# First slice of b on ScalarE's queue beside the rows of a, and its cast moved between the tiles of a

## The chip, the cores and the metric

One NeuronCore of a Trainium2 chip. The time is that of one execution on the device, in microseconds (us), median of several runs. "Span" is what the profile counts, from the first to the last instruction; it is about 1.8 us shorter than the time of the same execution (121.4 and 123.2).

## The reference

```python
m, k, n, p = 1024, 1024, 2048, 1024          # a: m x k, b: k x n, c: n x p, float32
h = np.matmul(a, b)
h = 0.5 * h * (1 + np.tanh(np.sqrt(2 / np.pi) * (h + 0.044715 * h ** 3)))
return np.matmul(h, c)
```

## The kernel before

The first half of a (four row tiles of 128 x 1024, 512 KB each) is loaded, cast to bf16 in halves by VectorE and ScalarE, transposed on TensorE and evicted in halves. Then the first product runs over eight slices of b (128 rows x 768 columns, 384 KB each), cast in halves by the same two engines. All these loads go out on SyncE's queue, a's four tiles first. Some small matmuls on zeros ("warm-ups") keep TensorE busy meanwhile. The rest of the kernel is untouched by the change.

```python
    def load_b0(k):
        st = b0stage.tile([128, W0], F32, name="b0_st")
        nc.sync.dma_start(out=st, in_=bv[:, k, 0:W0])
        b_st[k] = st
    ...
    for mt in range(4):
        load_a0(mt)                      # nc.sync
    for k in range(KT):                  # KT = 8
        load_b0(k)
    ...
    warm_up(8)                           # matmuls on zeros
    ...
    ab = [cast_a0(0)]                    # half on VectorE, half on ScalarE
    for mt in range(4):
        if mt < 3:
            ab.append(cast_a0(mt + 1))
        turn0(mt, ab[mt])                # 8 transposes; evictions: 4 on VectorE, 4 on ScalarE
        if mt < 3:
            warm_up(3)
    cast_b0(0)
    for k in range(KT):
        if k + 1 < KT:
            cast_b0(k + 1)
        for t in range(N0):              # N0 = 6
            nc.tensor.matmul(ps[t], bt(k, t), aT[0][:, k, :],
                             start=(k == 0), stop=(k == KT - 1))
```

## Time and profile before

| | before |
|---|---|
| time, median of 3 runs | 124.18 us (124.11 to 124.19) |
| time and span of the profiled execution | 123.2 us, 121.4 us |
| landings of a's tiles, as seen by VectorE's casts | 4.11, 5.37, 6.85, 8.14 |
| first matmul of the first product | 10.13 |
| landing of b's second slice | 10.89 |

A landing is read from the timeline: the start of the VectorE cast that waited for it.

### The profile page before, as it was taken

The numbers are of one execution on the slowest core, as the hardware profiler recorded it, in microseconds if no ns is written. First come the engines' busy times: TensorE is split into PE (matmuls) and PEld (weight loads), VectorE is DVE, ScalarE is ACT, GpSimd is POOL, SyncE is SP. The second block draws the span as 40 slices with busy tenths as digits, with TensorE's granted clock in tenths as the row PEclk, the third lists the DMA queues.
The fourth block names the chain that finished last, engine by engine and source line by source line (L and its number), as shares of the span: only waits on it lengthen the run. The fifth ranks groups of instructions, "written<-read, shape, count | busy, mean of one in ns | idle before, by whom it ended". The sixth has DMA issues, their size and how long they took to land.

```text
span 121.4 us, 1456 instructions
## 1 busy us (share of the span) xinstructions
PE 115.0 (95%) x562; PEld 67.2 (55%) x569; DVE 64.2 (53%) x94; ACT 30.8 (25%) x54; POOL 21.3 (18%) x26
## 2 busy tenths in 40 slices
PE   6897999999998999999999999999999999999980
PEld 2353444444456444444444444478888888888850
DVE  0354320000026000009999999999669999963440
ACT  4486535417311323332333233000000000000000
POOL 2000497134420400000000000994000000000000
PEclk9999999999999999999999999999999999999997
DMA  4999999999999999992000000002400024263443
GB/s 123 393 347 337 408 219 205 200 203 207 209 205 205 386 357 213 207 207 43 0 0 5 0 0 3 3 0 88 171 0 0 5 86 153 106 224 121 173 155 104
DMA packets 12150, 18.44 MB, mean 152 GB/s; under 512 B 752, under 2 KB 7152, under 8 KB 12144
## 3 DMA queue, kind: packets, MB, share of 16 engines
q0 software_dynamic: 7968, 8.91, 40.0%
q1 hardware_dynamic: 4176, 9.44, 21.0%
q8 instruction: 4, 0.07, 0.2%
q14 instruction: 2, 0.02, 0.0%
HBM read 20.97 MB, written 4.19 MB: 207 GB/s over the span
## 4 chain that ended last, share of the span: by engine, by line
PE 89%; DMA 4%; DVE 2%; issue 1%; SPq 1%; DVEq 0%
PE ps L267 41%; PE ps L164 31%; PE ps L136 9%; DMA a_st<-in_a_dram 4%; PE ps L155 3%; PE pt L155 3%; PE pt L183 1%; PE pt L111 1%; SPq L76 1%; DVE aT L114 1%; DVE aT L184 1%; PE ps L97 1%; DVE ab L103 0%; DVEq L362 0%; DVE b_lo L121 0%
## 5 line engine op out<-in xcount | busy, mean ns | idle before, releaser
L140 ACT ACTIVATE h<-ps 128x512 fp32r<-128x512 f32 (+1 forms) x30 | 17.3, 602 | 28.7 <-PE ps L164 26.3
L164 PE MATMUL ps<-aT,b_hi 128*128 128x512 bf16 x93 | 21.2, 379 | 0.2
L164 PE MATMUL ps<-aT,b_lo 128*128 128x512 bf16 x79 | 17.4, 379 | 0.1
L164 PEld LDWEIGHTS <-b_hi 128*128 128x128 bf16 x96 | 9.3, 98 | 10.9
L267 PE MATMUL ps<-t,s 128*128 128x512 f32 x64 | 15.1, 393 | 0.0
L267 PE MATMUL ps<-t,h 128*128 128x512 f32 x64 | 14.8, 389 | 0.0
L267 PE MATMUL ps<-c,h 128*128 128x512 bf16 (+2 forms) x71 | 14.1, 355 | 0.1
L267 PEld LDWEIGHTS ps<-t,s 128*128 128x128 f32 x64 | 12.0, 188 | 2.6
L267 PEld LDWEIGHTS ps<-t,h 128*128 128x128 f32 x64 | 12.0, 188 | 2.5
L307 POOL COPY lk<-u 128x512 f32<-128x512 f32 x1 | 7.5, 7492 | 33.6 <-ACT u L300 33.6
L164 PEld LDWEIGHTS <-b_lo 128*128 128x128 bf16 x80 | 7.8, 98 | 9.5
L221 DVE TENSOR_TENSOR t<-c,c 128x1024 fp32r<-128x1024 bf16 x4 | 4.7, 1222 | 15.6 <-ACT h L140 15.5
L184 DVE COPY aT<-pt 128x1024 bf16<-128x1024 bf16 x4 | 2.7, 689 | 19.4 <-PE pt L183 19.3
L136 PE MATMUL ps<-aT,b_lo 128*128 128x512 bf16 x47 | 10.3, 379 | 0.7 <-DVE b_lo L121 0.7
L267 PEld LDWEIGHTS <-h 128*128 128x128 bf16 x72 | 6.7, 98 | 7.4 <-issue 0.3
L209 POOL DMA_DIRECT2D c<-in_c_dram x8 | 5.9, 743 | 11.8 <-PE ps L164 6.0
L136 PEld LDWEIGHTS <-b_lo 128*128 128x128 bf16 x48 | 4.5, 98 | 6.1 <-DVE b_lo L121 0.8
L290 DVE TENSOR_TENSOR ot<-ps,u 128x512 f32<-128x512 f32 x11 | 7.3, 685 | 1.1 <-PE ps L267 1.1
L267 PE MATMUL ps<-c,s 128*128 128x512 f32 x32 | 7.4, 389 | 0.0
L97 PE MATMUL ps<-warm 128*128 128x512 bf16 x17 | 5.7, 476 | 1.2 <-DVE warm L49 1.2
L267 PEld LDWEIGHTS ps<-c,s 128*128 128x128 f32 x32 | 6.0, 188 | 1.2
L121 DVE CAST b_lo<-b_st 128x384 bf16<-128x384 f32 x8 | 2.9, 366 | 4.5 <-DMA b_st<-in_b_dram 4.5
(40 smaller groups left out, 95.1 us busy)
## 6 DMA issues: line engine op xcount, KB each, us to landing
out_dram<-ot SPq DMA_DIRECT2D x15, 256.0 KB, 2.0
b_st<-in_b_dram SPq DMA_DIRECT2D x8, 384.0 KB, 8.7
c<-in_c_dram POOLq DMA_DIRECT2D x6, 512.0 KB, 14.6
a_st<-in_a_dram SPq DMA_DIRECT2D x4, 512.0 KB, 4.7
c<-in_c_dram POOLq DMA_DIRECT2D x2, 1024.0 KB, 15.0
b_hi<-in_b_dram POOLq DMA_DIRECT2D x4, 384.0 KB, 11.3
b_lo<-in_b_dram POOLq DMA_DIRECT2D x2, 512.0 KB, 7.1
ab<-in_a_dram POOLq DMA_DIRECT2D x4, 256.0 KB, 13.9
```

The costliest lines, as they stand in the source:

```text
L97: nc.tensor.matmul(ps[N0 - 1], warm[:, 0:128], warm, start=True, stop=True)
L121: nc.vector.tensor_copy(b_lo[:, k, 0:HW], b_st[k][:, 0:HW])
L136: nc.tensor.matmul(ps[t], bt(k, t), aT[0][:, k, :], start=(k == 0), stop=(k == KT - 1))
L140: nc.scalar.activation(hq[h][t // NH][:, t % NH, :], p, AF.Gelu_apprx_tanh)
L155: nc.tensor.matmul(ps[t], bt(k + i, N0 + t), aT[0][:, k + i, :], start=(k + i == 0), stop=(k + i == KT - 1))
L164: nc.tensor.matmul(p, bt(k, t), aT[h][:, k, :], start=(k == 0), stop=(k == KT - 1))
L184: nc.vector.tensor_copy(aT[1][:, :, ts(j, 128)], pt)
L209: nc.gpsimd.dma_start(out=dst[:, t:t + 4, :], in_=cv[:, r * NH + t:r * NH + t + 4, ts(q, H)])
L221: nc.vector.tensor_tensor(t1[i], c12[:, ts(i, 2), :], c11[:, ts(i, 2), :], op=SUB)
L267: nc.tensor.matmul(p, lhs(t)[:, ts(j, 128)], rhs(t)[:, q], start=(t == 0), stop=(t == NH - 1))
L290: nc.vector.tensor_tensor(ot, u if swap else p, p if swap else u, op=op)
L307: nc.gpsimd.tensor_copy(last_keep, last)
```

## The change

The intent: b's first slice need not queue behind a, so its cast can be done while the engines wait for a, and nothing stands between the last eviction and the first matmul.

```diff
-    def load_b0(k):
+    def load_b0(k, queue=nc.sync):
         st = b0stage.tile([128, W0], F32, name="b0_st")
-        nc.sync.dma_start(out=st, in_=bv[:, k, 0:W0])
+        queue.dma_start(out=st, in_=bv[:, k, 0:W0])
 ...
+    load_b0(0, nc.scalar)
     for mt in range(4):
         load_a0(mt)
-    for k in range(KT):
+    for k in range(1, KT):
         load_b0(k)
 ...
     for mt in range(4):
         if mt < 3:
             ab.append(cast_a0(mt + 1))
+        if mt == 1:
+            cast_b0(0)
         turn0(mt, ab[mt])
         if mt < 3:
             warm_up(3)
-    cast_b0(0)
```

## The prediction

> **What bounds the kernel now.** I read the page first: the busy shares, the sliced picture, the chain that ended last.
>
> ```profile
> PE 115.0 (95%) x562; PEld 67.2 (55%) x569; DVE 64.2 (53%) x94; ACT 30.8 (25%) x54; POOL 21.3 (18%) x26
> PEclk9999999999999999999999999999999999999997
> PE 89%; DMA 4%; DVE 2%; issue 1%; SPq 1%; DVEq 0%
> ```
>
> TensorE works for 95% of the 121.4 us span and makes 89% of the chain, at a full clock until the last slice. What is left of the chain is mostly the head: 4% is a DMA of a. So a change to the head can only move the moment at which the dense stream of matmuls starts. I read the chain in order of time up to that moment (columns: start, length, what).
>
> ```profile
> 1.65 5.18 DMA a_st<-in_a_dram
> ...
> 7.67 0.73 PE pt L111 x8
> 8.40 0.65 PE ps L97 x3
> 9.05 0.30 PE pt L111 x4
> 9.35 0.02 issue
> 9.37 0.42 DVE aT L114
> 9.80 0.28 DVE b_lo L121
> 10.07 0.27 issue
> 10.35 10.33 PE ps L136 x47
> ```
>
> The reader is to see three things. The head is paced by the row tiles of a. After the last VectorE eviction of a transposed tile (9.37 to 9.80) the cast of b's first slice adds 0.28 us before the first weights can be loaded; this is what the change takes away. And the first matmul stage then runs without a hole: the row has 47 records where the code issues 48, and the timeline puts the first weight load at 10.12 with the first recorded matmul at 10.35, one step of 0.2155 us too late. So the missing record is the first matmul, at 10.13, and "0.27 issue" is no wait. 48 x 0.2155 = 10.34 us, to 20.48, where the next stage begins. From there the chain is TensorE almost to the end, with gaps of 0.05 us.
>
> The timeline shows what the last tile of a had to go through (start, length, engine, line, and in brackets the idle time before it):
>
> ```profile
> 8.14 0.63 ACT L104 ACTIVATE ab<-a_st 128x512 bf16<-128x512 f32 x1 [0.17 <-DMA a_st<-in_a_dram]
> 8.14 0.43 DVE L103 CAST ab<-a_st 128x512 bf16<-128x512 f32 x1 [0.53 <-DMA a_st<-in_a_dram]
> ...
> 8.48 0.42 DVE L114 COPY aT<-pt 128x512 bf16<-128x512 bf16 x1
> ...
> 8.95 0.74 PE L111 MATMUL pt<-ident,ab 128*128 128x128 bf16 x8
> ...
> 10.89 0.36 DVE L121 CAST b_lo<-b_st 128x384 bf16<-128x384 f32 x1 [0.83 <-DMA b_st<-in_b_dram]
> ```
>
> The casts of tile 3 wait for its landing; the eviction of tile 2 stands behind the cast in VectorE's order; the transposes of tile 3 need the bank that this eviction frees. Landing to first matmul is 10.13 - 8.14 = 1.99 us. The last row is the second slice of b, landed at 10.89. The same view has the other landings of a at 4.11, 5.37 and 6.85, and the third slice of b at 11.89.
>
> Last, the table by stretches (engine columns, then granted clock, DMA share, GB/s):
>
> ```profile
> 4.00:8.00 4.00, 3.47 (x28) 1.79 (x27) 1.95 (x5) 2.86 (x5) 0.00 (x0) 1.00 1.01 397
> 8.00:10.25 2.25, 1.69 (x16) 1.10 (x16) 1.45 (x4) 1.64 (x4) 0.00 (x0) 1.00 0.85 224
> ```
>
> While a is on its way the 16 DMA engines are full (share 1.01, 397 GB/s). There is a weak stretch, 8.00 to 10.25 at 224 GB/s, but it lies after a has landed, while the first two slices of b arrive. I don't know its cause.
>
> **What the Trainium skill says.** "DMA: Bandwidth & Descriptors", section "Issuing engines are not separate DMA queues": transfers started from different engines run on the same 16 DMA engines and interleave, and starting them from several engines "will only save the time on the sequencer it takes to initiate the DMA". The trace of before has only one such queue busy in the head, so it can't confirm the sharing; it does show full engines. The same page, "Queues, rings and completion order", says that a DMA engine goes round robin between the queues with work, packet by packet. No run yet shows that. "ScalarE: Activation LUTs", section "What ACT_TABLE_LOAD costs", gives about 1283 ns for the load; the trace has 1.28 us at 0.74, so it agrees. "TensorE: Matmul & The Clock Gate", section "HAM oscillation — how this bites in real kernels", warns of TensorE gaps above some 3.4 us; in before the clock stays at 1.00 with short gaps only.
>
> **The change part by part.**
>
> Issue. The first 384 KB slice of b is issued by ScalarE at its start, about 0.74, beside the first tile of a on SyncE. An issue takes some 0.4 us (median 0.42 for a's four). ScalarE's table load moves from 0.74 to about 1.2 and ends near 2.5, ahead of the first cast at 4.11 or later: free. SyncE issues one transfer less before the rest of b; its issues run ahead of the data anyway: free.
>
> Bytes. This is the cost. Before, b's slice came after the four tiles of a; now it shares the engines with tile 0, and every tile of a has these bytes in front of it. A slice of 384 KB at the pace of the later slices takes 11.89 - 10.89 = 1.00 us, at 397 GB/s 393 KB / 397 = 0.99 us. A little may be saved in the first half microsecond, where the engines are not full yet (the table by quarters of a microsecond has 147 and 279 GB/s between 2.00 and 2.50). I take a delay of 0.94 us for all four tiles: landings at 5.05, 6.31, 7.79, 9.08.
>
> Casts of b. Before, VectorE's half (0.35) stood between the last eviction and the first matmul. Now it goes between the cast of tile 2 and the eviction of tile 1. I walk it through with durations of before (VectorE cast 0.43, eviction 0.42, b 0.35; ScalarE 0.63, 0.58, 0.52; queued neighbours overlap by 0.08; 0.05 from an eviction to the transposes; 0.42 from the first of four transposes to the eviction).
> VectorE: cast of tile 2 at 7.79 to 8.22, b 8.14 to 8.49, eviction of tile 1 at 8.41 to 8.83. Then it waits for tile 3 at 9.08: the b cast is hidden.
> Tile 3: cast 9.08 to 9.51, eviction of tile 2 at 9.43 to 9.85, transposes from 9.90, eviction of tile 3 at 10.32 to 10.74, first matmul at about 10.79.
> ScalarE: cast of tile 2 to 8.42, b to 8.86, eviction of tile 1 to 9.36, cast of tile 3 from 9.27 (0.2 late) to 9.90, eviction of tile 2 to about 10.4, the second four transposes 10.45 to 10.7. These stand ahead of the first matmul on TensorE, but end before 10.79. ScalarE's last eviction, to about 11.45, is needed by the fifth step of the contraction only, 24 matmuls later.
>
> Sum: landing to first matmul is 10.79 - 9.08 = 1.71 in place of 1.99, a gain of 0.28; the landing is 0.94 later. Net 10.79 - 10.13 = 0.66 us later. The second slice of b keeps its place in the order of bytes (10.89 or earlier) and is needed at 10.79 + 6 x 0.2155 = 12.08: no stall. After that TensorE goes on as before, and later loads only get more slack. Some 0.1 may come back in the early DMA stretch, so I add 0.57: 124.18 + 0.57 = 124.75 us.
>
> **The rivals.**
>
> 1. The tiles of a are not delayed: the two queues fill the engines better, or the second queue gets its turn late. For it: the weak stretch of 224 GB/s shows that the engines can be made idle. Against it: in the stretch that matters they are full. Even then the gain is capped: the first matmul would come at 10.13 - 0.28 = 9.85, its seventh at 11.14, but the cast of b's second slice ends at 11.25 and gives weights at 11.31. That leaves 0.1 to 0.3 us: 123.9 to 124.1.
>
> 2. The weak stretch is bound to the clock time 8 to 10 us, or to the first reading of b, and now falls on the last tiles of a. It costs before about (397 - 224) x 2.25 = 389 KB, or 1 us of transfer. If half to all of it hits tile 3, the loss is 0.66 + 0.5 to 1.0: 125.3 to 125.8. For it: low rates begin with b's packets, and b now comes in with a. Against it: the later slices of b run at 412 GB/s, so b's rows as such aren't slow.
>
> 3. TensorE waits longer for tile 0 (warm-ups end at about 4.5, tile 0 lands at 5.05) and its clock falls back. The longest gap I get is 1.1 us, far from the skill's figure, so 5% at most; it would cost one to three microseconds.
>
> **Range and chances.** The middle is the byte argument, 124.75. Rival 1 gives the lower edge, 124.0; rival 2 the upper, 125.6. The three runs of before lie within 0.08 us, so noise adds little. Faster than 121.7 is impossible by removing 0.28 us: 1%. Slower than 126.66 needs rival 2 in full with rival 3: 2%. The same: 97%.
>
> **What would show it.** The first landing of a near 5.05 and the last near 9.08 confirm the byte argument; 4.1 and 8.1 refute it and point to rival 1. The chain should go from the eviction of the last tile straight to the matmuls, with no cast of b between. The casts of b's first slice should lie near 8.1, in idle time. A rate well under 397 GB/s before a has landed would be rival 2, a granted clock under 1.00 before 12 us rival 3. A hole in the first matmul stage would show a bound that I missed. Wrong altogether: a first matmul earlier than 9.8 or later than 11.6.

## The result, and the profile after

The changed kernel takes 125.70 us (median of 4 runs, 125.31 to 126.15) against 124.16 us of before in the same rounds. The ratio is 1.0126 (95% interval 1.0085 to 1.0166). Ratios here are the mean time of one kernel's runs over that of the other's of the same rounds, so not quite the ratio of the medians. It is slower by 1.54 us (125.70 - 124.16), just outside my range (124.0 to 125.6) and 0.95 us over my figure; by the 2% rule it counts as "same", as I expected.

From the page of the changed kernel: the granted clock in 40 slices, and the chain's shares.

```profile
PEclk9986999999999999999999999999999999999999
PE 89%; DMA 5%; DVE 2%; issue 1%; SPq 0%; DVEq 0%
```

The clock row has an 8 and a 6 in the third and fourth slice, that is from 6 to 12 us; before it was 9 there. The chain in order of time (start, length, what):

```profile
1.18 6.33 DMA a_st<-in_a_dram
...
8.34 1.01 PE pt L112 x8
9.36 1.28 PE ps L98 x3
10.64 0.85 PE pt L112 x8
11.49 0.72 PE ps L98 x3
12.21 0.24 PE pt L112 x4
12.45 0.02 issue
12.47 0.43 DVE aT L115
12.91 0.04 issue
12.95 0.38 PE ps L138
```

As intended, no cast of b stands between the last eviction and the first matmul. Yet the first matmul starts at 12.95, where before it was at 10.13, 2.82 us later. Eight transposes take 1.01 us and three warm-ups 1.28 (0.43 each), where before they took 0.73 and 0.65 (0.2155 each): TensorE runs at half speed there. The timeline has the landings of the four tiles of a:

```profile
5.94 0.43 DVE L104 CAST ab<-a_st 128x512 bf16<-128x512 f32 x1 [4.81 <-DMA a_st<-in_a_dram]
...
7.53 0.43 DVE L104 CAST ab<-a_st 128x512 bf16<-128x512 f32 x1 [1.16 <-DMA a_st<-in_a_dram]
...
8.81 0.43 DVE L104 CAST ab<-a_st 128x512 bf16<-128x512 f32 x1 [0.52 <-DMA a_st<-in_a_dram]
...
10.10 0.43 DVE L104 CAST ab<-a_st 128x512 bf16<-128x512 f32 x1 [0.26 <-DMA a_st<-in_a_dram]
```

I had predicted 5.05, 6.31, 7.79, 9.08: each is 0.9 to 1.2 us later than that. The table by stretches tells why (engine columns, then granted clock, DMA share, GB/s):

```profile
1.75:6.00 4.25, 3.04 (x8) 0.76 (x5) 0.06 (x1) 0.96 (x3) 0.00 (x0) 1.00 0.84 263
6.00:8.00 2.00, 1.27 (x11) 0.66 (x11) 0.84 (x3) 1.04 (x2) 0.00 (x0) 1.00 1.03 422
8.00:11.50 3.50, 3.16 (x20) 2.36 (x21) 2.15 (x6) 2.68 (x6) 0.00 (x0) 0.51 1.02 412
```

While b's first slice and a's first tile arrive, the engines move 263 GB/s; from 6 to 11.5 us they move 422 and then 412, through the rest of a and on into b's next slices. In before, the weak stretch lay at 8 to 10 us, where b's first slices arrived behind a. So a weak stretch now lies at the front, where b is read, and none at 8 to 10 us. And the granted clock is 0.51 from 8 to 11.5 us.

Two theories, then. Mine: three things add up, the bytes of b in front of a, the weak stretch that goes with the first reading of b, and the half clock. Rivals: two queues that share the engines are slow by themselves; or the weak stretch is bound to something else than b.

### The profile page after: what moved, and what is told of

Same layout as the page of the kernel before. It is cut to its first block, busy times and chain, and to the rows that moved or that the text cites. A ratio compares the mean times of both kernels' runs of the same rounds, so it can differ in the third digit from the quotient of the medians. Undisturbed runs are those within 1.5% of the kernel's fastest.

```text
span 124.2 us, 1456 instructions
## 1 busy us (share of the span) xinstructions
PE 116.3 (94%) x562; PEld 68.3 (55%) x569; DVE 64.3 (52%) x94; ACT 30.3 (24%) x54; POOL 18.6 (15%) x26
## 4 chain that ended last, share of the span: by engine, by line
PE 89%; DMA 5%; DVE 2%; issue 1%; SPq 0%; DVEq 0%
PE ps L269 40%; PE ps L166 30%; PE ps L138 8%; DMA a_st<-in_a_dram 5%; PE ps L157 3%; PE pt L157 3%; PE pt L112 2%; PE ps L98 2%; PE pt L185 1%; DVE aT L115 1%; DVE aT L186 1%; DVE ab L104 0%; SPq L76 0%; DVEq L364 0%; DVE ot L338 0%
## 5 line engine op out<-in xcount | busy, mean ns | idle before, releaser
L138 PE MATMUL ps<-aT,b_lo 128*128 128x512 bf16 x47 | 10.5, 379 | 0.3 <-DVE aT L115 0.3
L309 POOL COPY lk<-u 128x512 f32<-128x512 f32 x1 | 4.8, 4774 | 33.3 <-ACT u L302 33.3
L98 PE MATMUL ps<-warm 128*128 128x512 bf16 x17 | 6.8, 550 | 1.2 <-DVE warm L49 1.2
L112 PE MATMUL pt<-ident,ab 128*128 128x128 bf16 x32 | 3.3, 265 | 2.3 <-DVE ab L104 1.6
```

Source lines behind the costliest of these rows:

```text
L98: nc.tensor.matmul(ps[N0 - 1], warm[:, 0:128], warm, start=True, stop=True)
L112: nc.tensor.transpose(pt[:, k, :], ab[:, ts(4 * g + k, 128)], ident)
L138: nc.tensor.matmul(ps[t], bt(k, t), aT[0][:, k, :], start=(k == 0), stop=(k == KT - 1))
L309: nc.gpsimd.tensor_copy(last_keep, last)
```

## The experiments

All times in us; "last tile" is the landing of a's fourth tile, "first matmul" that of the first product, both from the profile. Where the first record is missing (the first weight load lies 0.23 us ahead of the first recorded matmul), I took 0.2155 off.

| kernel | last tile | first matmul | span of the profile | median time | ratio to before (95%) |
|---|---|---|---|---|---|
| before, first profile | 8.14 | 10.13 | 121.4 | 124.16 | |
| changed kernel | 10.10 | 12.95 | 124.2 | 125.70 | 1.0126 (1.0085 to 1.0166) |
| before_again | 8.28 | 10.27 | 121.6 | 124.02 | 0.9981 (0.9938 to 1.0024) |
| before_look | 8.56 | 10.54 | 122.8 | 124.49 (2 runs) | 1.0029 (1.0005 to 1.0052) |
| after_warm | 10.09 | 12.15 | 123.4 | 125.25 | 1.0087 (1.0060 to 1.0114) |
| queue_only | 10.15 | 12.14 | 123.4 | 125.26 | 1.0089 (1.0074 to 1.0104) |
| one_queue | 10.38 | 12.87 | 124.2 | 126.06 | 1.0157 (1.0114 to 1.0200) |
| dummy_a | 9.19 | 11.17 | 122.4 | 124.21 | 1.0014 (0.9990 to 1.0038) |
| cast_only | 9.04 | 10.77 | 122.0 | 124.03 | 0.9988 (0.9962 to 1.0014) |
| a_two_queues | 8.20 | 10.43 | 121.7 | 123.64 | 0.9956 (0.9929 to 0.9983) |
| a_queues_warm | 8.18 | 10.17 | 121.6 | 123.61 | 0.9962 (0.9938 to 0.9987) |
| touch | 8.97 | 10.97 | 122.2 | 123.93 | 0.9977 (0.9960 to 0.9993) |
| touch_rows | 8.64 | 10.62 | 121.9 | 123.53 | 0.9957 (0.9926 to 0.9989) |
| touch_far | 8.65 | 10.64 | 121.9 | 123.51 | 0.9954 (0.9914 to 0.9994) |
| touch_a | 8.89 | 10.87 | 122.1 | 123.81 | 0.9975 (0.9934 to 1.0016) |
| combined | 8.44 | 10.42 | 121.7 | 123.61 | 0.9966 (0.9919 to 1.0013) |
| slice_twice | 9.38 | 11.37 | 122.6 | 124.43 (1 run) | |

**The clock: after_warm.** The changed kernel with more warm-ups ahead of the first tile.

```diff
-    warm_up(8)
+    warm_up(15)
```

> The changed kernel with 15 warm-up matmuls before the first tile in place of 8, so that TensorE has no gap of 1.6 us before the first tile of a. Theory clock: the gap brings the half clock from about 8 to 11.5 us and costs about 1 us in executions that have it; expect clock 1.00 throughout the head, first matmul of b about 1 us earlier than 12.95 (11.8 to 12.0), time 124.9 to 125.3 with less spread than 125.3 to 126.2. Rival (all of the loss is the landing of a): the time stays 125.3 to 126.2.

Measured: 125.25 (125.21 to 125.30), first matmul at 12.15, 0.15 us past the range that I expected. Its table by stretches:

```profile
1.75:6.00 4.25, 4.25 (x15) 1.49 (x12) 0.09 (x1) 0.98 (x3) 0.00 (x0) 1.00 0.84 266
8.00:11.50 3.50, 2.89 (x27) 1.90 (x28) 2.07 (x6) 3.23 (x7) 0.00 (x0) 1.00 1.02 413
```

TensorE's first busy column is full now in the first stretch (4.25 of 4.25, where the changed kernel had 3.04), and the clock stays at 1.00 where it was 0.51. The column can't be trusted before about 4 us, though: it shows 1.00 there too, while the weight loads of the warm-ups come 0.43 us apart (from 1.60 to 3.73 in before and in the changed kernel), the pace of the warm-ups in the stretch of 0.51. The weak stretch is the same (266 against 263 GB/s), and the last tile lands at 10.09 against 10.10. So the half clock is a cost of its own: 12.95 - 12.15 = 0.80 us in the profiled execution and 0.45 us in the medians, since not every run of the changed kernel has it (mean clocks 0.986, 0.986, 0.996 and 1.000 with times 125.97, 126.15, 125.43 and 125.31). More than 1 us over before remains.

**One queue: one_queue.** The changed kernel, with b's first slice still first, but on SyncE's queue.

```diff
-    load_b0(0, nc.scalar)
+    load_b0(0, nc.sync)
```

> The changed kernel with b's first slice still first, but on SyncE's queue ahead of a, so that one queue serves all. Theory first reading: the weak stretch goes with the first megabyte of b that is read, so it stays at the start (rates under 330 GB/s between 2 and 6 us), last tile of a near 10.1. Theory two queues: the weak stretch comes from two queues that share the engines, so it is gone here: engines full at 390 to 410 GB/s, last tile of a near 9.1, time about 124.7 if the clock holds. Theory clock time (the stretch lies at 8 to 10 us whatever is read): it hits the last tile of a.

Measured: 126.06, last tile at 10.38, and between 1.75 and 6 us

```profile
1.75:6.00 4.25, 2.63 (x8) 0.76 (x5) 0.00 (x0) 0.47 (x2) 0.00 (x0) 1.00 0.91 270
```

270 GB/s with one queue, 263 with two. The weak stretch needs no second queue, and "clock time" falls as well: between 8 and 10 us this kernel is at 395 to 424 GB/s in every half microsecond. The half clock is here too (mean 0.983 in the profiled run), so the time of 126.06 holds both costs.

**Two queues without b: a_two_queues.** Before, with a's second tile on ScalarE's queue.

```diff
     def load_a0(mt):
         st = astage.tile([128, K], F32, name="a_st")
-        nc.sync.dma_start(out=st, in_=av[:, mt, :])
+        (nc.scalar if mt == 1 else nc.sync).dma_start(out=st, in_=av[:, mt, :])
```

> The kernel before with nothing moved but the second tile of a, which ScalarE's queue issues, beside the first tile on SyncE's queue. Order of bytes of b as before. Theory two queues: a weak stretch appears between 2 and 5 us, the last tile of a lands 0.5 to 1 us later than 8.14. Theory first reading of b: rates of 390 to 410 GB/s until a has landed, last tile at 8.1, the weak stretch stays with b's first slices at 8 to 10 us; first tile lands later (about 5.3, together with the second), the time is within 0.3 us of before.

Measured: 123.64 (123.49 to 123.72), last tile at 8.20; the casts of the first two tiles run back to back from 5.48. The table:

```profile
2.50:8.00 5.50, 4.30 (x28) 1.98 (x27) 2.04 (x5) 2.68 (x6) 0.00 (x0) 1.00 1.01 403
8.00:10.25 2.25, 1.86 (x21) 1.21 (x19) 1.38 (x4) 1.75 (x4) 0.00 (x0) 1.00 0.91 277
```

Two queues on a alone run at 403 GB/s, and the weak stretch stays behind a, with b (277 GB/s, somewhat milder). The rival of two queues falls. This kernel is even 0.4% faster than before.

**The bytes without b: dummy_a.** Before, with 384 KB of a's later rows, unused, first on ScalarE's queue, and 15 warm-ups.

```diff
+    spare = consts.tile([128, W0], F32, name="spare")
+    nc.scalar.dma_start(out=spare, in_=av[:, 4, 0:W0])
     for mt in range(4):
         load_a0(mt)
 ...
-    warm_up(8)
+    warm_up(15)
```

> The kernel before, with 384 KB that nobody uses put first on ScalarE's queue in the place where the change puts b's first slice, but taken from rows of a (row tile 4), and 15 warm-ups for the clock. It has the bytes of the change without reading b early. Byte argument: the last tile of a lands 0.95 to 1.0 us later than 8.14, near 9.1, with the engines at 390 to 410 GB/s from 2.5 us on. Then the other 1 us of the change's delay (10.09) belongs to reading b early. Rival (any two queues with these bytes are slow): last tile near 10.1 and rates of 200 to 340 between 2 and 6 us. First matmul at about 11.1 in the first case; time 124.6 to 125.0.

Measured: last tile at 9.19, first matmul at 11.17.

```profile
1.75:6.00 4.25, 4.25 (x13) 1.52 (x11) 0.43 (x1) 1.53 (x3) 0.00 (x0) 1.00 0.97 345
```

345 GB/s, start included, where reading b in the same place gives 263. The byte argument of my prediction (9.08) is right to 0.1 us for bytes that are not b's: the delay is 9.19 - 8.14 = 1.05. The other 10.09 - 9.19 = 0.90 us of the changed kernel's delay comes from reading b so early. (What in b does it is not separated: b's rows also lie 8 KB apart and a's 4 KB. But b's later slices, with the same rows, reach 412 GB/s.) The time, 124.21, is a miss: I expected 124.6 to 125.0, as first matmuls at 11.17 and 10.13 differ by 1.04, and found no difference to before at all. This pointed to the timed runs of before: they may lose about 1 us that its first profile doesn't show.

**The kernel before again: before_again and before_look.** No edit (before_look has one more comment line).

> The kernel before, unchanged, for a second profile. The first profile of before was of an execution about 1 us shorter (123.2) than its timed runs (124.1 to 124.2). If something in the timed runs of before costs this 1 us, a second profile should show it: either half clock in the head, or the weak stretch of the DMA engines lying on a's tiles. If the second profile equals the first (last tile of a at 8.1, first matmul at 10.1, clock 1.00), the 1 us was chance. Ratio to before 1.000 +- 0.003.

> The kernel before, unchanged, one more profile. Three kernels that leave a's transfers as in before (one touch, one slice twice, cast alone) showed a's third tile at 7.75 to 8.09 in their profiles, one of the 16 DMA engines a tile behind, where the two profiles of before have 6.85 and 7.00. Theory: this also happens in most timed runs of before, whose spans are 122.0 to 122.6 where the profiled ones are 121.4 and 121.6. If this profile falls in such a run: third tile at 7.7 to 8.1, first matmul near 11, span 122.0 to 122.6. If the span is over 122 with the third tile at 7.0, the theory falls.

The first gave another short execution (123.36 us, span 121.6; timed 123.36 to 124.32). The second fell in a long one (124.54 us, span 122.8). Its timeline:

```profile
7.29 0.43 DVE L103 CAST ab<-a_st 128x512 bf16<-128x512 f32 x1 [1.22 <-DMA a_st<-in_a_dram]
...
10.54 1.49 PE L136 MATMUL ps<-aT,b_lo 128*128 128x512 bf16 x6 [0.43 <-DVE b_lo L121]
...
11.85 0.36 DVE L121 CAST b_lo<-b_st 128x384 bf16<-128x384 f32 x1 [1.37 <-DMA b_st<-in_b_dram]
...
12.27 1.04 PE L136 MATMUL ps<-aT,b_lo 128*128 128x512 bf16 x4 [0.24 <-DVE b_lo L121]
...
21.86 0.61 PE L155 MATMUL pt<-aT,b_lo 128*128 128x512 bf16 x2 [0.35 <-DMA b_lo<-in_b_dram]
```

The third tile of a is late by 0.44 us (7.29 against 6.85), less than the 7.7 to 8.1 that I expected, so my theory held in part only. The rest was new: b's second slice lands at 11.85 in place of 10.89, and the product stops after six matmuls. They start at 10.54 and would hand over at 10.54 + 6 x 0.2155 = 11.83; the seventh starts at 12.27. That is 0.44 us of hole, and 0.41 us of later start, together 0.85. The rest of span 122.8 - 121.4 = 1.4 is a second hole: the other 42 matmuls would hand over at 12.27 + 42 x 0.2155 = 21.32, but the next stage (L155) starts at 21.86, when its own load of b has landed. GpSimd issues that load only after the fifth slice of b (the copy to `gate`), which came at 14.83 here and at 13.88 in the first profile. So 0.41 + 0.44 + 0.54 = 1.39 us. The clock is 1.00 in this stretch.

Before thus has longer and shorter executions, and no clear border between them: 32 timed runs lie between 123.55 and 124.55, the profiled ones at 123.2, 123.36 and 124.54. In the long one that I could look into, the head is held up by the loads of b: the weak stretch (207 GB/s from 8 to 10.25 us, against 224 and 255 in the two short ones) delays b's second slice by 0.96 us, more than the later start and the slack of 0.11 us can take up. The changed kernel has neither hole in its profile. That the timed runs lose time in the same way is likely, but one profile doesn't show it. I had predicted from a short one.

**The cast alone: queue_only and cast_only.** queue_only is the changed kernel with 15 warm-ups and the cast back at its old place. cast_only is before with the cast moved between the last two evictions, later than the place that the change gives it (`mt == 1`); so it isn't quite the other half of the change.

```diff
 queue_only, against after_warm             cast_only, against before
-        if mt == 1:                        +        if mt == 3:
-            cast_b0(0)                     +            cast_b0(0)
         turn0(mt, ab[mt])                           turn0(mt, ab[mt])
+    cast_b0(0)                             -    cast_b0(0)
```

> One part alone: b's first slice first on ScalarE's queue, but its casts left at the old place behind the last eviction; 15 warm-ups, so that the clock holds as in the kernel with 15 warm-ups and both parts (125.25, first matmul at 12.15). My step of the prediction that the moved cast is worth 0.28 us: first matmul at 12.4, time about 125.5. Rival (the cast in the middle delays ScalarE and gives the gain back): first matmul at or before 12.15, time 125.2 or less.

> The other part alone: queues and order of transfers as in before, b's first slice cast between the last two evictions, where VectorE would wait for the slice at 9.14. First matmul at about 9.9 in place of 10.13, but the seventh needs the second slice, landed at 10.9 and cast at 11.25: a hole of about 0.15 us there, gain 0.1 us: 124.1. If the weak stretch is longer in the timed runs than in the profiles, no gain at all.

queue_only: 125.26, first matmul at 12.14 (weight load at 12.13, the first record missing). after_warm: 125.25, at 12.15. Moving the cast to this place is worth nothing: my 0.28 us is not there, and the rival of the expectation holds. (In queue_only the warm-ups kept the pace of 0.43 us until 6.7, so the first transposes started at 7.32 in place of 6.40; by tile 1 they are within 0.1 us of each other, 8.42 and 8.34.) The timeline of after_warm shows where it goes:

```profile
9.34 0.51 ACT L123 ACTIVATE b_lo<-b_st 128x384 bf16<-128x384 f32 x1
...
9.75 0.58 ACT L117 ACTIVATE aT<-pt 128x512 bf16<-128x512 bf16 x1
...
9.88 0.88 PE L112 MATMUL pt<-ident,ab 128*128 128x128 bf16 x8 [0.16 <-DVE aT L115]
...
10.60 0.81 PE L98 MATMUL ps<-warm 128*128 128x512 bf16 x3
...
11.25 0.61 PE L112 MATMUL pt<-ident,ab 128*128 128x128 bf16 x8
```

ScalarE's half of the cast of b (9.34) pushes its eviction of tile 1 to 9.75 to 10.33. The second four transposes of tile 2 need that bank, so they end late; the three warm-ups stand behind them in TensorE's order (10.60), and the transposes of tile 3 behind those (11.25). In queue_only, whose landings are 0.06 us later, the same transposes start at 10.97. What VectorE saves at the end is spent by ScalarE in the middle. The warm-ups' part in it is read from this trace; no run takes them out with the cast in the middle.

cast_only: 124.03, ratio 0.9988 with 1 in the interval: no gain seen in the time. In its profile the third tile of a was late (7.78), so its first matmul at 10.77 can't be set against the 9.9 of the expectation. But landing to first matmul can: 10.77 - 9.04 = 1.73 us, against 1.99 in before. Between the last two evictions, where VectorE and ScalarE both wait (0.47 us each in before), the moved cast does save 0.26 us of the chain. So it was its place ahead of tile 1's eviction that gave the gain back.

**The weak stretch: touch, touch_rows, touch_far, touch_a, slice_twice.** All are before with one extra read: small in the four touches, a second copy of b's first slice (384 KB) in slice_twice. The four touches are issued by ScalarE at the start: 16 rows x 64 bytes over b's first 2 MB; 256 rows x 64 bytes of b's first two slices; the same of b's last two slices; the same of rows of a.

```diff
 touch
+    nc.scalar.dma_start(out=touch, in_=b.rearrange("(r s) n -> r s n", s=16)[0:16, 0, 0:16])
 touch_rows        in_=bv[:, 0:2, 0:16]
 touch_far         in_=bv[:, 6:8, 0:16]
 touch_a           in_=av[:, 6:8, 0:16]
 slice_twice, behind the load of slice 0
+            nc.sync.dma_start(out=again, in_=bv[:, 0, 0:W0])
```

> The kernel before, with one tiny extra read at the start, issued by ScalarE: 16 rows of b, 64 bytes of each, 128 KB apart, so that they span the memory of b's first two slices (2 MB). Theory cold address: the weak stretch is the cost of first reading an address range, so after the touch the stretch of 215 to 320 GB/s between 8 and 10 us is gone or much shorter, b's second slice lands near 10.1 in place of 10.9, and timed runs settle near 123.4 to 123.7 instead of 123.7 to 124.4. Theory row pitch (the 16 engines start b's 8 KB pitched rows in step and hamper each other until they drift apart): the touch changes nothing, second slice at 10.9, time 124.2.

> The kernel before with a larger early touch of b: 64 bytes of each of the first 256 rows (two slices), 16 KB in 256 packets, on ScalarE's queue at the start. Theory of an address that must be read once by the same engine: the weak stretch between 8 and 10 us is gone, the second slice lands near 10.1. Theory that it takes some 200 packets or 3 us from the first reading of b: gone too, since 256 packets and 5 us have passed. Theory that only full-length rows of b do it (a row pitch effect at the start of the stream): stretch stays, second slice at 10.9 or later. In the first two cases a's first tile should be late by 0.3 to 1 us.

> As the touch of 256 rows (123.53, second slice landed at about 10.5, rates of 300 to 344 between 8 and 10 us), but the touched rows are those of b's last two slices, whose long reads come 6 us later. Theory that the touched addresses must be the ones read next: the stretch is back as in before (170 to 270 GB/s for 2 us, second slice at 10.9 to 11.8), time 124.0 to 124.4. Theory that any early reading of b in 256 packets does it: rates of 300 or more, time 123.4 to 123.7.

> The same touch in shape and place, but of rows of a that nobody needs then. If the gain of the touch has nothing to do with b (for instance the small packets space out the engines' work on a), the time is 123.4 to 123.7 here too and the rates between 8 and 10 us are 300 or more. If it is the reading of b, the time stays at 124.0 to 124.4, with the stretch of before.

> The kernel before, which reads b's first slice twice in a row, the second copy unused (a look; it is slower by the bytes). Theory cold address: the second copy of the same addresses runs at full rate and the weak part comes back with the second slice, that is later than in before. Theory row pitch or start of a stream: the second copy takes the weak part and the second slice then runs at full rate. Either way the second slice lands about 1 us later than in before, at 11.9, and the first matmul stage has a hole of some 0.5 to 0.8 us.

The rates from 8.00 to 10.25 us (last column of each row of the table by stretches) were 208 with touch, 323 with touch_rows, 263 with touch_far and 228 with touch_a; the three profiles of before had 224, 255 and 207. So one profile, that of touch_rows, shows the stretch clearly milder, with b's second slice by 10.6 (not the 10.1 expected, and a's first tile at 4.16 was not late). touch, at 123.93 with the second slice at 11.40, fits neither of its two theories. But the times don't follow: touch_far, with the stretch hardly changed, is as fast (123.51) as touch_rows (123.53), against the expectation of 124.0 to 124.4, and touch_a's interval overlaps both. slice_twice (one run, state unknown) moved 395 GB/s from 7.5 to 9 us, 238 from 9 to 10.5 and 385 from 10.5 to 12: the unused second copy of the same addresses was in the weak part, and the new addresses of the second slice, behind it, mostly were not, as the second theory of the expectation had it. A cost of reading each address for the first time would look the other way round, so that theory is out in its plain form. What makes the engines slow for some two to four microseconds once b is read stays open; the pitch of b's rows at the start of its stream was not tested apart from b. That it comes with the first reading of b's slices, on one queue or two, early or late, is what one_queue, a_two_queues, dummy_a and before show together.

**A faster version: a_queues_warm and combined.** a_queues_warm is a_two_queues with other warm-ups; combined adds the touch of touch_rows behind a's second tile.

```diff
-    warm_up(8)
+    warm_up(12)
 ...
-        if mt < 3:
-            warm_up(3)
+        if mt < 2:
+            warm_up(2)
```

> Candidate for a faster version: the second tile of a on ScalarE's queue (123.64, first matmul 10.43, held by TensorE's own warm-ups between the tiles), with 12 warm-ups first, 2 after the first two tiles and none after the third. The chain from the last landing (8.20) should be 1.75 to 2.0 as in before: first matmul at 10.0 to 10.2, then a hole of up to 0.2 us at the seventh matmul for b's second slice. Time 123.3 to 123.5 if the clock holds. Rival: the clock falls without the warm-ups, 124 or more.

> Candidate: the second tile of a on ScalarE's queue with the changed warm-ups (123.61), and behind it on that queue the touch of 256 rows of b. If the two repairs add up (first matmul near 10.2 and the second slice by 10.6, no hole at the seventh matmul), 123.2 to 123.4. If the touch only takes from a what it gives to b: 123.5 to 123.8.

The first matmul came to 10.17 as expected, yet the time stayed at 123.61, against 123.64 for a_two_queues and my 123.3 to 123.5. Of the 0.26 us that the first matmul gained, 0.10 is left at the start of the next stage (20.70 against 20.80). The fourth matmul loses 0.11 us, as its weights wait for ScalarE's half of the cast of b (loaded at 10.93; it would start at 10.17 + 3 x 0.2155 = 10.82). The next stage loses some 0.08 more against 10.17 + 0.11 + 10.34 = 20.62. b's second slice, landed at 11.06, holds nothing up. combined has 123.61 too, so the two don't add up. The best found, a_two_queues, touch_rows and touch_far, beat both kernels by a small margin: ratios 0.9954 to 0.9957 to before, each interval below 1. By the 2% rule they too are "same", and they are the best of several tries.

## Why the prediction was wrong, point by point

**The bound and what the change can move: right for the execution that was profiled.** From the first matmul on, both profiles run alike: the first matmul is 2.82 us later and the span 124.2 - 121.4 = 2.8 us longer. "Without a hole" does not hold for the long execution of before. And "at a full clock until the last slice" was a wrong reading: the warm-ups up to 3.7 us run at the half pace of 0.43 us.

**"I take a delay of 0.94 us for all four tiles": the term that failed.** It measured 10.10 - 8.14 = 1.96. Byte for byte I was right: with bytes of a in that place the delay is 1.05 (dummy_a). But I let b's bytes move at the pace of later slices, although the profile showed b's first slices in a weak stretch. The stretch came along with b, and 0.9 us of it came to lie before a. This was my second rival, which I gave the upper edge of the range, 125.3 to 125.8, and not the middle. "For it: low rates begin with b's packets" was the right reading.

**"The b cast is hidden", gain 0.28: wrong.** Landing to first matmul was to be 1.71. With the clock held it measured 12.15 - 10.09 = 2.06, and 1.99 with the cast at its old place (queue_only). I walked ScalarE's delay through, but left the three warm-ups out of TensorE's order between the transposes of tiles 2 and 3. They are 3 x 0.2155 = 0.65 us, and behind a late eviction they push tile 3. The gain became a loss of 0.07. The size was right for another place: cast_only keeps 0.26 of it.

**The clock, rival 3, "5% at most": wrong.** The gap that I foresaw, 1.1 us, became about 1.6 with the later landing (warm-ups end at 4.8, the first transposes start at 6.43), and half clock followed in the profiled run (1.64 us before the transposes, then 0.65). It cost 0.80 us there and 0.45 in the medians, less than the "one to three microseconds" of the prediction.

**The base: missed.** I took the difference from a profile of a short execution (123.2) and added it to the median of longer ones (124.16), which may have lost about 1 us to waits for b that the change takes away.

**The sum in the profiles.** 0.66 predicted, 1.02 more from the landing (1.96 - 0.94), 0.35 from the cast and the warm-ups (2.06 - 1.71), 0.79 from the clock (2.85 - 2.06, where 2.85 = 12.95 - 10.10): 2.82, as measured. **In the medians** the difference is 1.54. The profiled executions differ by 125.97 - 123.2 = 2.77; the changed kernel's median is 0.27 under its profiled run, before's is 0.96 over its own: 2.77 - 0.27 - 0.96 = 1.54. So my figure came out nearer than its reasoning: two errors, about 1.4 us of the first two terms and 0.45 of the clock, were partly cancelled by a base that was 1 us too short. That it came within 1 us is luck.

**What would show it.** The signs that I named worked. The landings near 5.9 and 10.1 refuted the size, a rate far under 397 named rival 2, and a clock under 1.00 named rival 3.

## What to carry to other kernels

A transfer put at the front costs its bytes to all that follows, and it may bring a slow start with it, as b's first slice did: look at the rate at which it runs where it is now before you give it a pace. Put a moved instruction into every engine's order, with the fillers that stand there too, before you call it hidden. And compare the time of the profiled execution with the median first: if they differ by as much as the effect that you estimate, the profile is of one end of the spread, and other waits may bind at the other end.

## What the Trainium skill lacked or had wrong

- "TensorE: Matmul & The Clock Gate", section "HAM oscillation — how this bites in real kernels": it warns of gaps above some 3.4 us. In the changed kernel's profile a gap of 1.64 us (to 6.43) and another of 0.65 us (to 8.34) were enough: clock 0.51 from 8.0 to 11.5 us. With the first gap filled by warm-ups (after_warm) it stayed at 1.00, with a gap of 0.67 us to 8.34 left. It isn't sure to happen: two of the changed kernel's four runs had mean clocks of 0.996 and 1.000, as those of before (0.994 to 1.000).
- "DMA: Bandwidth & Descriptors", section "Issuing engines are not separate DMA queues": that two queues share the engines is borne out (casts of a's first two tiles back to back from 5.48, last tile at 8.20, where one queue had 8.14). With one tile of a on the second queue the kernel took 123.64 in place of 124.20, ratio 0.9956 (0.9929 to 0.9983). This does not show the page wrong: SyncE's issues of b start at 2.10 us there and at 2.59 in before, so the saved issue time may be the cause; it was not tested apart.
- No page that I read has the slow start of b: 263 GB/s over 4.25 us when b is read first (270 with one queue; 345 with a's rows in its place), 207 to 255 over 2.25 us in before, where it comes behind a, against 397 to 422 otherwise. Its cause is open.
